# The first block's second map by seven over quarter blocks, its sums of weights made once, and opening loads in 4 KB rows

## The chip, the cores and the metric

The kernel runs on one core of one Trainium2 chip. The metric is the device time of one execution in microseconds (us). The kernel before took 1738.44 us as the median of three runs, from 1736.94 to 1740.64.

## What is computed

One decoder layer on x of 1 x 2048 x 1024 in float32: a token-mixing half (one input projection, a short causal convolution on one part, causal pooling over four windows on the other, one output projection), then an MLP with squared ReLU, each half with a DeepNorm residual and a LayerNorm, and each modulated by a vector that comes from c.

```python
mod = silu(c) @ w_ada + b_ada            # sh1, sc1, g1, sh2, sc2, g2
h = x * (1 + sc1) + sh1
z = h @ w_in
mix = concat(gate_b * short_conv(gate_c * v_conv), pool(v_pool)) @ w_out
x = layer_norm(ALPHA * x + (1 + g1) * mix)
h = x * (1 + sc2) + sh2
f = square(relu(h @ w_mlp_in)) @ w_mlp_out      # 1024 -> 4096 -> 1024
x = layer_norm(ALPHA * x + (1 + g2) * f)
```

The first map of the MLP is `w_mlp_in`, the second is `w_mlp_out`.

## The kernel before

**Tiling.** The 2048 tokens are two blocks of 1024 (b = 0 and 1). Every operand of a matmul is split into a high part in fp32r and a low part that holds the rest, and `mm3` (L84 to L87) makes three matmuls of it: high by high, high by low, low by high. So one tile step of a product costs three matmuls of 128 x 512 (L85, L86, L87). The split is one cast on ScalarE (ACT, L80) and one subtraction on VectorE (DVE, L81). Products of blocks are made by the scheme of Winograd's seven: seven products of half blocks in the place of eight, on operands that are sums and differences of blocks. Those sums are made on DVE (L90), and those of weights are kept in DRAM.

**Stages.** The stages follow one another: the opening (loads, modulation of the first k), the input projection of block 0 (`first_group`, L392, then the rest), its output projection, its first map (`up`, eight groups g of seven products each), its second map (`down`), and then the same for block 1.

**The first map.** Each group of `up` (L964) issues seven products. A product has 24 matmuls, 12 for each of two PSUM banks. The products go to three pairs of banks, X, Y and Z. Product 0 writes X. Then `keep` (L973, two ACT copies of 128 x 512) takes X into the tile c11. Product 2 then adds to X, and `keep` takes it into c12, product 4 adds to X once more. Products 1 and 5 write Y or Z and are added with `add` to what was kept (L90 on DVE, two adds of 128 x 512). `join` puts ReLU (L982) and square (L983) on ACT behind that. What results goes to DRAM (`usum`, L989, by GpSimd's queue, POOL), in block 1 also as the sums of its quarter blocks: `save_quarters` (L946), four DVE sums of 128 x 256 and three stores (L952, L954, L959) into `uquart`, done for two of the tiles of each group. All these tiles come from one pool, o, of ten slots; in block 0 one of them holds the conditioning row until the second map, so nine turn round.

**Sums of weights.** Between the groups of `up`, `sum_blocks` (L930) and `sum_weights` (L500) make sums of weights for later stages, a half at a time: four loads of 256 KB into two o tiles, four DVE sums of 128 x 512, four stores of 256 KB. `HALF_SUMS` says how many half-sums stand behind each group of block 0. Block 1 makes eight more, one behind each group (into `wquart`, L941).

**The second map.** `down` (L1068) takes the seven products in steps of half a product (96 matmuls of 512 columns). In block 0 it has all seven products as 14 such steps. In block 1 products 1 and 5 are left out of these steps, and each is made by seven again over quarter blocks (14 products of 48 matmuls of 256 columns in all, L1104), from `uquart` and `wquart`. Beside the steps of block 0 stand the sums of the next block's inputs (`sum_x`), the residual, and the gate row g2 (`row_of`).

**What sets the order.** A scheduler puts the instructions of every engine into one fixed order, by priority and by the pool slots that it expects to be free; an engine executes its list in that order and waits at the head of it. SyncE (SP) issues the loads in order, POOL the stores. At the start, `in_turn` (L97) chains the opening loads, the conditioning vector is spread over the partitions by eight transposes (L133), seven warm-up matmuls follow (L146), `ada_first` (L175) makes the modulation of k = 0, and `shifted` (L208) applies it on ACT.

## Time and profile before

| what | value |
|---|---|
| median of three runs | 1738.44 us (1736.94 to 1740.64) |
| profiled execution | 1739.93 us, of which the span is 1738.1 us |
| mean granted clock of TensorE | 0.997 |
| TensorE (PE) busy | 1721.4 us, 99% of the span |
| DVE, ACT, POOL busy | 77%, 51%, 13% |
| DMA | 479.42 MB, mean 276 GB/s |

Busy times say how full an engine was, not what the end waited for. Here PE is full from one end to the other, so a change in the time is either fewer or shorter matmuls, or a change in the few places where PE stands. For those the list of waits by engine and line is read, and for the cause of one the timeline of the engine that it waited for. Times in a timeline are from the start of the span.

### The profile page before, as it was taken

The numbers are of one execution on the slowest core, as the hardware profiler recorded it, in microseconds if no ns is written. First come the engines' busy times: TensorE is split into PE (matmuls) and PEld (weight loads), VectorE is DVE, ScalarE is ACT, GpSimd is POOL, SyncE is SP. The second block draws the span as 40 slices with busy tenths as digits, with TensorE's granted clock in tenths as the row PEclk, the third lists the DMA queues.
The fourth block names the chain that finished last, engine by engine and source line by source line (L and its number), as shares of the span: only waits on it lengthen the run. The fifth ranks groups of instructions, "written<-read, shape, count | busy, mean of one in ns | idle before, by whom it ended". The sixth has DMA issues, their size and how long they took to land.

```text
span 1738.1 us, 22312 instructions
## 1 busy us (share of the span) xinstructions
PE 1721.4 (99%) x7966; PEld 1438.7 (83%) x7966; DVE 1341.7 (77%) x1753; ACT 880.1 (51%) x1190; POOL 232.6 (13%) x437
## 2 busy tenths in 40 slices
PE   8999999999999999999999999999999999999997
PEld 7888888888888888888888888887888888998886
DVE  7898697877777686669686789687767768887885
ACT  5323358554445555446573344774545555773551
POOL 0212221112232000000000000103222221000000
PEclk9999999999999999999999999999999999999999
DMA  9898877778888999787672366557765589998871
GB/s 376 320 337 324 313 251 276 257 276 304 321 328 312 382 419 342 291 301 245 214 261 79 117 226 214 209 197 270 252 247 200 212 311 393 381 359 330 282 254 49
DMA packets 149583, 479.42 MB, mean 276 GB/s; under 512 B 17632, under 2 KB 18144, under 8 KB 149472
## 3 DMA queue, kind: packets, MB, share of 16 engines
q1 hardware_dynamic: 102816, 313.88, 50.1%
q0 software_dynamic: 46656, 164.13, 24.7%
q8 instruction: 62, 1.02, 0.2%
q14 instruction: 49, 0.40, 0.1%
HBM read 328.51 MB, written 149.42 MB: 275 GB/s over the span
## 4 chain that ended last, share of the span: by engine, by line
PE 93%; issue 2%; DMA 2%; DVE 1%; ACT 0%; POOL 0%; SPq 0%; DVEq 0%; POOLq 0%; ACTq 0%
PE ps L85 28%; PE ps L86 28%; PE ps L87 28%; PE ps L1104 5%; PE ps L392 3%; PE ps L743 1%; DMA usum<-o 1%; DVE o L90 1%; DMA r<-in_w 0%; DMA o<-in_wins 0%; DMA r<-in_win 0%; DVE o L1300 0%; DVE o L1294 0%; DMA w2sum<-o 0%; DVE st L712 0%
## 5 line engine op out<-in xcount | busy, mean ns | idle before, releaser
L85 PE MATMUL ps<-h,w 128*128 128x512 f32 x1312 | 510.1, 389 | 1.4 <-ACT o L973 1.4
L87 PE MATMUL ps<-h,w 128*128 128x512 f32 x1312 | 510.3, 389 | 0.1
L86 PE MATMUL ps<-h,w 128*128 128x512 f32 x1312 | 510.3, 389 | 0.0
L85 PE MATMUL ps<-h,h 128*128 128x512 f32 x992 | 386.3, 389 | 0.0
L87 PE MATMUL ps<-h,h 128*128 128x512 f32 x992 | 386.1, 389 | 0.0
L86 PE MATMUL ps<-h,h 128*128 128x512 f32 x992 | 386.0, 389 | 0.0
L80 ACT CAST h<-r 128x1024 fp32r<-128x1024 f32 (+1 forms) x196 | 199.3, 1021 | 283.5 <-PE ps L86 143.5
L81 DVE TENSOR_TENSOR h<-r,h 128x1024 fp32r<-128x1024 f32 (+1 forms) x196 | 230.8, 1182 | 83.9 <-ACT h L80 81.0
L85 PEld LDWEIGHTS ps<-h,w 128*128 128x128 f32 x1312 | 246.0, 188 | 53.3 <-ACT o L973 1.8
L87 PEld LDWEIGHTS ps<-h,w 128*128 128x128 f32 x1312 | 246.2, 188 | 51.6 <-DVE w L81 0.5
L86 PEld LDWEIGHTS ps<-h,w 128*128 128x128 f32 x1312 | 246.3, 188 | 51.5 <-DVE h L81 0.5
L80 ACT CAST w<-r 128x1024 fp32r<-128x1024 f32 x156 | 164.1, 1052 | 236.7 <-PE ps L86 230.4
L81 DVE TENSOR_TENSOR w<-r,w 128x1024 fp32r<-128x1024 f32 x156 | 190.4, 1221 | 78.9 <-ACT w L80 78.6
L90 DVE TENSOR_TENSOR o<-o,o 128x1024 f32<-128x1024 f32 (+2 forms) x218 | 186.6, 859 | 52.4 <-DMA usum<-o 45.4
L87 PEld LDWEIGHTS ps<-h,h 128*128 128x128 f32 x992 | 186.2, 188 | 38.9
L85 PEld LDWEIGHTS ps<-h,h 128*128 128x128 f32 x992 | 186.2, 188 | 38.7 <-DVE o L862 0.2
L86 PEld LDWEIGHTS ps<-h,h 128*128 128x128 f32 x992 | 186.2, 188 | 38.4
L81 DVE TENSOR_TENSOR h<-w,h 128x1024 fp32r<-128x1024 f32 x124 | 151.2, 1219 | 9.0 <-ACT h L80 9.0
L90 DVE TENSOR_TENSOR o<-o,ps 128x512 f32<-128x512 f32 (+1 forms) x172 | 111.7, 664 | 40.7 <-PE ps L87 39.8
L80 ACT CAST h<-w 128x1024 fp32r<-128x1024 f32 x124 | 130.1, 1049 | 12.1 <-DMA w<-in_w 7.1
L989 POOL DMA_DIRECT2D usum<-o x96 | 51.4, 536 | 419.4 <-DVE o L90 144.5
L90 DVE TENSOR_TENSOR r<-r,r 128x1024 f32<-128x1024 f32 x60 | 73.4, 1223 | 28.3 <-DMA r<-in_w 25.3
(145 smaller groups left out, 1419.0 us busy)
## 6 DMA issues: line engine op xcount, KB each, us to landing
usum<-o POOLq DMA_DIRECT2D x96, 512.0 KB, 5.5
r<-usum SPq DMA_DIRECT2D x96, 512.0 KB, 5.6
w<-w2sum SPq DMA_DIRECT2D x64, 512.0 KB, 6.3
r<-in_w SPq DMA_DIRECT2D x60, 512.0 KB, 6.0
o<-in_w SPq DMA_DIRECT2D x72, 256.0 KB, 6.5
w2sum<-o POOLq DMA_DIRECT2D x64, 256.0 KB, 6.6
w<-in_w SPq DMA_DIRECT2D x32, 512.0 KB, 6.6
r<-uquart SPq DMA_DIRECT2D x28, 512.0 KB, 6.0
```

Of the source, the lines that this page charges most:

```text
L80: high = nc.scalar.copy(hi, src)
L81: return high.ins, nc.vector.tensor_tensor(lo, src, hi.bitcast(F32), op=ALU.subtract).ins
L85: nc.tensor.matmul(ps, whi, xhi, start=first, stop=False, skip_group_check=goes_on)
L86: nc.tensor.matmul(ps, whi, xlo, start=False, stop=False, skip_group_check=goes_on)
L87: nc.tensor.matmul(ps, wlo, xhi, start=False, stop=last, skip_group_check=goes_on)
L90: return nc.vector.tensor_tensor(out_, a, b_, op=op)
L392: nc.tensor.matmul(ps[m, h], wt[:, w : w + P], A[k][p // 2][:, hs], start=k == 0 and p == 0, stop=k == KD - 1 and p == 2)
L743: nc.tensor.transpose(ps[:, t * P : t * P + P], R[4 * h + t][:, k * P : k * P + P], ident)
L989: nc.gpsimd.dma_start(usum[g, i], r)
L1104: nc.tensor.matmul(ps, a[:, us], w[:, gs], start=not begun, stop=hf == 1 and g == 3 and a is ul, skip_group_check=True)
```

## The change

Four things are changed.

1. Block 0's second map takes the form of block 1's: ten steps for products 0, 2, 3, 4 and 6, and 14 products over quarter blocks (L1122 now) for products 1 and 5. So block 0's first map saves quarter sums too, and the work beside the steps (residual, `sum_x`, `row_of`) moves to earlier steps.
2. The eight half-sums of `wquart` are made once, in block 0's first map, and block 1 makes none.
3. The opening loads are three of 512 KB with rows of 4 KB, from a new input `opening` that the host lays out, and one of 256 KB. Before they were seven of 256 KB with rows of 2 KB. `ada_first` goes by halves of the row.
4. Four warm-up matmuls on zeros stand ahead of the spread of the conditioning vector, and 14 behind it (seven before).

The diff, cut to its core:

```diff
-HALF_SUMS = (1, 2, 3, 3, 3, 3, 3, 0)
-WARM = 7
+HALF_SUMS = (2, 3, 4, 4, 4, 4, 4, 1)
+EARLY, WARM = 4, 14
...
-    for hs in halves:
-        for i, f in enumerate((SC1, SH1)):
-            in_turn(first[i][:, hs], wada[f][:, hs])
-    in_turn(w0[:, :H], win0[0])
-    for hs in halves:
-        in_turn(x0[:, hs], xT[0, 0][:, hs])
+    for r, src in zip((first[0], first[1], w0), opening):
+        in_turn(r, src)
+    in_turn(x0[:, H:], xT[0, 0][:, H:])
+    zeros = t_tmp()[:, :P]
+    nc.vector.memset(zeros, 0.0)
+    warm = t_ps()
...
+    warming(EARLY)
...
-    warm = t_ps()
-    for _ in range(WARM):
-        nc.tensor.matmul(warm[:, :P], ident, ident, start=True, stop=True)
+    with tc.issue_after(spreads[-1]):
+        warming(WARM)
...
         def save(r, i):
-            if fine and i in (1, 7):
+            if i in (1, 7):
                 save_quarters(r, i // 4, g)
...
-        coarse = (0, 2, 3, 4, 6) if b else (0, 1, 2, 3, 5, 4, 6)
-        steps = [(i, hf) for i in coarse for hf in range(2)]
+        steps = [(i, hf) for i in (0, 2, 3, 4, 6) for hf in range(2)]
...
-            if b and n == 1:
+            if n == 1:
                 made = [fine_operands(*todo[m]) for m in range(2)]
...
-            if n == base:
+            if n == 2:
                 next(later)
-            if base <= n < base + 4:
+            if 2 <= n < 6:
                 later.send(ready[1])
...
-            if b == 0 and n == 4:
+            if b == 0 and n == 2:
                 row_of(g2, mod[:, G2 : G2 + KD])
...
-        else:
-            sums = [(sum_blocks, [w2q[n, i, hf] for i in range(4)], wquart[n, hf], p)
-                    for n in range(2) for hf in range(2) for p in halves]
+            sums += [(sum_blocks, [w2q[n, i, hf] for i in range(4)], wquart[n, hf], p)
+                     for n in range(2) for hf in range(2) for p in halves]
...
-            some = 1 if b else HALF_SUMS[g]
+            some = HALF_SUMS[g]
```

**How the instructions move.** The first place is ACT's list in block 0's first map, group g = 4. The names: o_571 is c11 of this group before, o_579 its c12, o_584 its c22; w_580, w_585 and w_587 are the high parts of the weights of products 3, 4 and 5, and a w tile's slot comes free when an earlier product has been made. Before:

```order
L80 CAST w_580_3803<-r_576_3767 128x1024 [waits PE_49]
L973 COPY o_571_3729<-ps_569_3703 128x512 [waits DMASW4_49,DVE_49]
L973 COPY o_571_3729<-ps_570_3716 128x512 [waits PE_49]
L982 ACTIVATE o_571_3729<-o_571_3729 128x1024 [waits DVE_49]
L80 CAST w_585_3836<-r_565_3693 128x1024 [waits PE_49]
L983 ACTIVATE o_571_3729<-o_571_3729 128x1024 [waits Activation_49]
L973 COPY o_579_3800<-ps_569_3703 128x512 [waits DMASW6_49,PE_49]
L80 CAST w_587_3869<-r_564_3692 128x1024 [waits PE_49]
L973 COPY o_579_3800<-ps_570_3716 128x512 [waits PE_49]
```

In the changed kernel o_588 is c11 of the same group, o_596 its c12 and o_601 its c22, and w_597, w_602 and w_604 belong to products 3, 4 and 5:

```order
L80 CAST w_597_3925<-r_593_3889 128x1024 [waits PE_49]
L80 CAST w_602_3958<-r_582_3815 128x1024 [waits DVE_49,PE_49]
L80 CAST w_604_3991<-r_581_3814 128x1024 [waits DVE_49,PE_49]
L982 COPY o_588_3851<-ps_586_3825 128x512 [waits DMASW5_49,DMASW3_49,DVE_49]
L982 COPY o_588_3851<-ps_587_3838 128x512
L982 COPY o_596_3922<-ps_586_3825 128x512 [waits DMASW5_49,DMASW4_49,DMASW6_49,DVE_49,PE_49]
L982 COPY o_601_3955<-ps_599_3929 128x512 [waits DMASW6_49,DMASW7_49,DMASW0_49,DVE_49]
L982 COPY o_601_3955<-ps_600_3942 128x512
L991 ACTIVATE o_588_3851<-o_588_3851 128x1024 [waits DVE_49]
L80 CAST w_607_4030<-r_583_3816 128x1024 [waits DMAHW6_49,PE_49]
L992 ACTIVATE o_588_3851<-o_588_3851 128x1024 [waits Activation_49]
L982 COPY o_596_3922<-ps_587_3838 128x512 [waits PE_49]
```

The copies that free X for product 2 have moved from ahead of the casts for products 4 and 5 to behind them, and the second copy of c12, which frees X for product 4, now stands behind ReLU and square of c11. The cast of w_604 waits for the end of product 3. PE's list has turned round with it: in groups 2 to 7 it makes the products in the order 0, 1, 3, 2, 4, 5, 6, before in the order 0 to 6. The same rows in the same order stand in groups 3 to 7.

The second place is DVE's list in the same group of the changed kernel, the last rows ahead of what the ReLU of c11 waits for (the second row of o_588). The tiles o_576 to o_579 are half-sums of weights, the low part of product 5's weights is w_605, and ps_591 and ps_592 are the banks of Y:

```order
L90 TENSOR_TENSOR o_576_3785<-o_576_3785 128x512 [waits DMAHW1_49,DMAHW0_49,DMASW4_49]
L81 TENSOR_TENSOR w_605_3992<-r_581_3814,w_604_3991 128x1024 [waits PE_49,Activation_49]
L90 TENSOR_TENSOR o_576_3785<-o_576_3785,o_577_3786 128x512 [waits DMAHW2_49,DVE_49]
L90 TENSOR_TENSOR o_588_3851<-o_588_3851,ps_591_3858 128x512 [waits DMASW3_49,Activation_49]
L90 TENSOR_TENSOR o_577_3786<-o_576_3785,o_577_3786 128x512 [waits DMASW7_49,DMASW6_49,DVE_49]
L90 TENSOR_TENSOR o_578_3799<-o_578_3799 128x512 [waits DMAHW5_49,DMAHW4_49,DMASW0_49]
L90 TENSOR_TENSOR o_577_3786<-o_577_3786 128x512 [waits DMAHW3_49,DVE_49]
L90 TENSOR_TENSOR o_578_3799<-o_578_3799,o_579_3800 128x512 [waits DMAHW6_49,DVE_49]
L90 TENSOR_TENSOR o_588_3851<-o_588_3851,ps_592_3871 128x512 [waits Activation_49]
```

From the quarter sums of the group before (the tile o_571) to the last of these rows there are 18 DVE instructions in a row: 14 sums of half-sums, two low parts of weights, and the two adds. Before, the adds of c11 stood among such sums too, but product 3 stood between the copies of c12 and product 4, which needs them; now product 4 follows product 2 at once.

The third place is the head of PE's list, up to the first matmul of the input projection (L392 before, L401 now). Before:

```order
L133 MATMUL ps_94<-ident,silu 128x128 x4
L133 MATMUL ps_99<-ident,silu 128x128 x4
L146 MATMUL ps_104<-ident 128x128 x7
L392 MATMUL ps_184<-h_161,w_160 128x512
L392 MATMUL ps_186<-h_161,w_160 128x512
```

And now:

```order
L119 MATMUL ps_79<-tmp_77 128x128 x4
L141 MATMUL ps_98<-ident,silu 128x128 x4
L141 MATMUL ps_103<-ident,silu 128x128 x4
L119 MATMUL ps_79<-tmp_77 128x128 x14
L401 MATMUL ps_194<-h_171,w_170 128x512
```

Seven more matmuls stand between the spread and the first matmul of the input projection, and four ahead of the spread.

More of the change, by code (lines that the diff above doesn't have):

```diff
@@ L42, in tile_hybrid_layer @@
 @with_exitstack
-def tile_hybrid_layer(ctx: ExitStack, tc: tile.TileContext, xT, x, wada, vec, win0, win,
+def tile_hybrid_layer(ctx: ExitStack, tc: tile.TileContext, opening, xT, x, wada, vec, win0, win,
                       wins, wpool, wout, wmix, w1, w2, w2q, rows, out):
@@ L109, in tile_hybrid_layer, with warming @@
     w0 = t_r()
-    for hs in halves:
-        for i, f in enumerate((SC1, SH1)):
-            in_turn(first[i][:, hs], wada[f][:, hs])
-    in_turn(w0[:, :H], win0[0])
-    for hs in halves:
-        in_turn(x0[:, hs], xT[0, 0][:, hs])
+    for r, src in zip((first[0], first[1], w0), opening):
[4 more added lines that the diff above has]
+    warm = t_ps()
+    def warming(n):
+        for _ in range(n):
+            nc.tensor.matmul(warm[:, :P], zeros, zeros, start=True, stop=True)
+    warming(EARLY)
     silu = cp.tile([P, KD], F32, name="silu")
@@ L1233, in down @@
             banks, new, then = table[i]
-            matmuls(banks, ops, new, hf == 0, hf == 1, then, hf == 1 and i in by_tile)
-            if b and n == 1:
+            matmuls(banks, ops, new, hf == 0, hf == 1, then, hf == 1 and i in (3, 4, 6))
+            if n == 1:
                 for m, (k, part_) in enumerate(todo):
@@ L1331, in mlp @@
     def mlp(b, B, back, g2):
-        ups = [up(g, B, b == NB - 1) for g in range(NC)]
+        ups = [up(g, B) for g in range(NC)]
         for g in range(2):
```

52 lines of the change are left out of this document (26 added, 26 removed).

## The prediction

> **What bounds the kernel now.** I read the page's engine shares first, then PE's waits by releaser, then the chain and the timelines of the places named there.
>
> ```profile
> span 1738.1 us, 22312 instructions
> PE 1721.4 (99%) x7966; PEld 1438.7 (83%) x7966; DVE 1341.7 (77%) x1753; ACT 880.1 (51%) x1190; POOL 232.6 (13%) x437
> ```
>
> PE's waits (microseconds in total, times, longest):
>
> ```profile
> PE ps L133 <- DVE silu L90: 3.1, 1, 3.1
> PE ps L392 <- ACT h L209: 3.0, 1, 3.0
> PE ps L85 <- ACT o L973: 1.4, 1, 1.4
> ```
>
> PE is full, and the three waits sum to 7.5 us: two in the opening, one in block 1. So little is to be won beside matmuls saved, and any new wait of PE counts in full. The third wait shows the kind. Its PE rows, then ACT's rows (start, length, what, idle before and its releaser), then the row of the chain that holds block 1's quarter products:
>
> ```profile
> 1180.75 0.39 PE L85 MATMUL ps<-h,w 128*128 128x512 f32 x1
> ...
> 1183.93 0.39 PE L87 MATMUL ps<-h,w 128*128 128x512 f32 x1
> 1185.71 0.50 PE L85 MATMUL ps<-h,w 128*128 128x512 f32 x1 [1.40 <-ACT o L973]
> ```
>
> ```profile
> 1184.13 1.04 ACT L80 CAST w<-r 128x1024 fp32r<-128x1024 f32 x1 [4.38 <-PE ps L86]
> 1185.08 2.04 ACT L973 COPY o<-ps 128x512 f32<-128x512 f32 x4
> ```
>
> ```profile
> 1474.33 80.63 PE ps L1104 x672
> ```
>
> Fourteen steps from 1180.75 to 1183.93 are 0.227 us a matmul. Then 1.78 pass to the next start, so 1.56 are lost: a cast that waits for the end of product 3 stands ahead of the copy that frees the bank, and the copy starts only behind it.
>
> **The change part by part.** The sum is made on the profiled execution, 1739.93 us (span 1738.1 and 1.8 around it). That is 1.5 above the median of the runs, so my prediction takes the sum's difference from 1738.4.
>
> *Quarter products in block 0.* Products 1 and 5 leave as 4 steps of 96 matmuls: 384 x 0.227 = 87.2 us. In come 672 matmuls of 256 columns, 80.6 by the row of L1104. PE is the bound there, so **-6.5**.
>
> *Opening.* PE's rows, ACT's rows, and three stretches (PE, PEld, DVE, ACT, POOL busy, granted clock, DMA share, GB/s):
>
> ```profile
> 4.83 2.28 PE L146 MATMUL ps<-ident 128*128 128x128 f32 x14
> 10.14 22.19 PE L392 MATMUL ps<-h,w 128*128 128x512 f32 x84 [3.03 <-ACT h L209]
> ```
>
> ```profile
> 9.27 1.52 ACT L209 ACTIVATE h<-o,mod 128x512 fp32r<-128x512 f32 x2
> 15.10 1.52 ACT L209 ACTIVATE h<-o,mod 128x512 fp32r<-128x512 f32 x2 [1.48 <-DVE mod L191]
> ```
>
> ```profile
> 4.00:6.00 2.00, 2.00 (x11) 2.00 (x10) 1.39 (x4) 0.00 (x0) 0.00 (x0) 1.00 0.74 211
> 12.00:14.00 2.00, 2.00 (x6) 1.60 (x5) 2.00 (x4) 0.62 (x1) 0.00 (x0) 0.50 1.03 419
> 16.00:18.00 2.00, 2.00 (x10) 1.61 (x9) 1.46 (x3) 2.00 (x4) 0.00 (x0) 0.94 1.04 422
> ```
>
> The opening's 2 KB rows moved 211 GB/s, the 4 KB rows of the later loads 419. So the modulation should be ready about a microsecond earlier. But PE has 14 warm-up matmuls now in the place of 7: 4.83 + 2 x 2.28 = 9.39 is the earliest start of the input projection, 0.75 before 10.14. After PE's gap of 3.03 the clock was at half, still so from 12 to 14, and near full again from 16 on: the first 84 matmuls took 22.19 where 84 x 0.227 = 19.1, so 3.1 were lost. With PE busy from the spread on I expect the full clock. What is late next is k = 1: its ACT step stood at 15.10, and product 0 would end at 9.39 + 24 x 0.227 = 14.8; with loads a microsecond earlier it is up to 0.6 late. So -0.75 - 3.1 + 0.5 = **-3.3**, bounds -0.7 (no clock gained) and -3.9.
>
> The Trainium skill ("TensorE: Matmul & The Clock Gate", Part 1, What's actually happening) says that the clock falls after an idle window of about 3.4 us, and that the window runs free. The trace differs: a gap of 3.03, shorter than a window, halved it. By the page's rule 3.03 would have cost nothing and the half clock came from the phase, so the change might keep it: the sum would be 3.1 higher.
>
> *Block 1's first map.* Eight half-sums less. PE is the bound, so only the wait above can go; there the copy now stands ahead of the cast. **-1.4**, bounds -1.6 and 0.
>
> *Block 0's first map.* This is the large term. The same order that cost 1.56 once now stands in five groups, g = 3 to 7: casts for products 4 and 5, then the copies of c11, while product 2, which needs them, follows product 3. So 1.56 a group is the least. The second copy of c12, which the second half of product 4 needs, is later still. For it I walk one group on rows of block 1 (same saves, one half-sum) and then of block 0, group 4. T is the start of the cast for product 2, which the last matmuls of the group before release; products end at T + 5.44 each.
>
> ACT, DVE and POOL of a group in block 1:
>
> ```profile
> 1316.38 1.06 ACT L80 CAST w<-r 128x1024 fp32r<-128x1024 f32 x1 [1.85 <-PE ps L86]
> ...
> 1321.82 1.05 ACT L80 CAST w<-r 128x1024 fp32r<-128x1024 f32 x1 [2.80 <-PE ps L86]
> ```
>
> ```profile
> 1323.94 1.23 DVE L90 TENSOR_TENSOR o<-o,o 128x1024 f32<-128x1024 f32 x1 [3.18 <-DMA usum<-o]
> 1325.09 1.22 DVE L81 TENSOR_TENSOR w<-r,w 128x1024 fp32r<-128x1024 f32 x1
> 1326.22 0.76 DVE L90 TENSOR_TENSOR o<-o 128x256 f32<-128x256 f32 x2
> 1326.89 0.88 DVE L90 TENSOR_TENSOR o<-o,o 128x256 f32<-128x256 f32 x2
> 1327.69 1.28 DVE L90 TENSOR_TENSOR o<-o,ps 128x512 f32<-128x512 f32 x2
> 1328.89 0.69 DVE L90 TENSOR_TENSOR o<-o 128x512 f32<-128x512 f32 x1
> 1329.49 1.22 DVE L81 TENSOR_TENSOR w<-r,w 128x1024 fp32r<-128x1024 f32 x1
> 1330.62 1.41 DVE L90 TENSOR_TENSOR o<-o,o 128x512 f32<-128x512 f32 x2
> ```
>
> ```profile
> 1326.17 0.58 POOL L954 DMA_DIRECT2D uquart<-o  x1
> ```
>
> Issues by kind in the DMA view of 1310 to 1350 (KB each, median us to landing), and ACT of block 0, group 4:
>
> ```profile
> o<-in_w2q SPq DMA_DIRECT2D x4, 256.0 KB, 7.0
> uquart<-o POOLq DMA_DIRECT2D x2, 128.0 KB, 5.8
> ```
>
> ```profile
> 429.97 1.06 ACT L80 CAST w<-r 128x1024 fp32r<-128x1024 f32 x1 [1.18 <-PE ps L86]
> ...
> 445.25 1.06 ACT L982 ACTIVATE o<-o 128x1024 f32<-128x1024 f32 x1 [7.27 <-DVE o L90]
> 446.22 1.03 ACT L80 CAST w<-r 128x1024 fp32r<-128x1024 f32 x1
> 447.15 1.06 ACT L983 ACTIVATE o<-o 128x1024 f32<-128x1024 f32 x1
> 448.12 0.56 ACT L973 COPY o<-ps 128x512 f32<-128x512 f32 x1
> ```
>
> The last subtraction on c11 waits for a store and starts at T + 7.6, and the quarter sums end at 1327.69 = T + 11.3. Behind them the new order has 14 sums and two adds of 128 x 512 (0.60 from 1328.89 to 1329.49) and two low parts (1.13 from 1329.49 to 1330.62): 16 x 0.60 + 2 x 1.13 = 11.9, so the last add ends at T + 23.2 if its loads are there. The last pair of loads needs the slot of the tile whose quarter store is issued at 1326.17 (T + 9.8): + 5.8 + 7.0 = T + 22.6, with two DVE steps behind it T + 23.8. Then ReLU, cast, square and copy, 445.25 to 448.68 = 3.4: the copy ends at T + 27.2. Without any wait PE would want that bank at T + 21.8 + 2.7 = T + 24.5. So 2.7 a group, and more as the DMA fills: I take 3.0, between 1.56 and 5.
>
> ```profile
> 409.00:447.00 38.00, 37.94 (x168) 31.08 (x166) 27.89 (x33) 17.22 (x21) 9.76 (x20) 1.00 0.83 306
> ```
>
> Each more half-sum adds 2.1 MB, the quarter saves 0.7: 306 + 2.8 MB / 38 us = 380 GB/s, share 1.0, where the opening's later stretch moved 419. Five groups make 15. Group 1 has block 1's pattern, 1.56, and group 2, with three half-sums, I put at 1.5 (0 to 3). **+18**, bounds +8 (five times 1.56, nothing in groups 1 and 2) and +29.
>
> The Trainium skill ("DMA: Bandwidth & Descriptors", Specifications) gives a core about 358 GB/s from HBM; the trace does not hold to it (419). By 358 each of the five groups would take 38.1 x 380 / 358 = 40.4 at least, 2.3 more, which lies below the wait found above and would change no sign.
>
> *Block 0's second map.* Four of its steps have the loads of `sum_x` and of the residual together now; before, these stood beside different steps. A step of block 0 with `sum_x` and one of block 1 with the residual:
>
> ```profile
> 626.00:648.00 22.00, 22.00 (x99) 18.22 (x98) 16.93 (x19) 12.45 (x15) 1.07 (x2) 1.00 1.03 418
> 1577.00:1599.00 22.00, 22.00 (x98) 18.21 (x98) 16.58 (x16) 8.27 (x9) 1.07 (x2) 1.00 0.91 330
> ```
>
> `sum_x` adds 2.1 MB in 22 us to the 330 GB/s of the second row: 425, as full as the first, where PE was busy throughout. At 419 a step would be 0.3 us longer, and loads land later; **+1**, bounds 0 and +4 (one us a step).
>
> Sum: -6.5 - 3.3 - 1.4 + 18 + 1 = +7.8, so 1747.7 by the profiled execution and **1746.2** by the median. A measurement of this kernel can't tell less than about 0.2% (3.5 us) from no change.
>
> **The rivals.** *The cover holds (0.21).* If the DVE row is through earlier than I walked it, the wait behind the cast is the only one left: 5 x 1.56 = 7.8 and -6.5 - 3.3 - 1.4 + 7.8 = -3.4, 1735; if in some groups the casts run before product 3 ends, down to 1727. That is faster than before. It decides at T + 22.6: a ReLU of c11 that starts by then adds nothing to the 1.56. For it speaks that in block 0 before, c11's ReLU started at 445.25, T + 15.3; against it, that the quarter sums and the fourth half-sum (1.47 + 4 x 0.60, and the subtraction behind a store) stand ahead of it now, and that the cast for product 5 cannot start before product 3 ends.
>
> *DMA-bound first map (0.15).* With share 1.0 stores and loads land 2 to 3 us later each; both stand in the chain above, so 5 a group and more: 25 + 6 + 4 - 11.2 = +24, 1762. It decides where groups 3 to 7 move above 400 GB/s.
>
> *No clock gained in the opening (0.12).* If the half clock comes again, the opening gives 0.7, and the sum is +10.4, 1749. The Trainium skill ("TensorE: Matmul & The Clock Gate", Part 1, What's actually happening) would allow it by the phase of its window.
>
> **How the numbers follow.** The forecast (waits of 2 to 4 us in five groups, 1738 to 1753) has 0.52, of which 0.14 lies within 0.2% (up to 1741.9). The first rival's 0.21 is 0.04 within it and 0.17 below 1734.9. So faster 0.17, same 0.18, and slower 0.38 + 0.15 + 0.12 = 0.65. The range of 1733 to 1758 leaves out some 0.1 of the first rival and 0.1 of the second.
>
> **What would show it.** In the profile after: a wait of PE (L85) on ACT's copy (L982), five to seven times, some 15 us in all; groups 3 to 7 of block 0's first map 40 to 42 us long; the quarter products twice at 80.6; the first matmul of the input projection at 9.4 and the clock at 1.00 until 20 us; no such wait in block 1. The prediction is wrong if PE shows no wait on L982, or if those groups are 38.1 us long.

## The result and the profile after

| kernel | us, median (lowest to highest) | runs |
|---|---|---|
| before | 1739.54 (1736.94 to 1741.67) | 4 |
| after | 1807.06 (1800.47 to 1808.37) | 4 |

The ratio is 1.0381 with a 95% interval of 1.0351 to 1.0412: the changed kernel is slower by 67.5 us, where I had forecast 7.8. The page of the changed kernel (profiled execution 1808.23 us, mean granted clock 0.982), then PE's waits (microseconds in total, times, longest):

```profile
span 1806.3 us, 23209 instructions
PE 1741.8 (96%) x8276; PEld 1463.6 (81%) x8276; DVE 1399.7 (77%) x1858; ACT 905.2 (50%) x1222; POOL 257.4 (14%) x469
```

```profile
PE ps L85 <- ACT o L982: 40.2, 12, 5.2
PE ps L86 <- DVE h L81: 6.3, 1, 6.3
PE ps L1112 <- ACT o L1122: 3.9, 1, 3.9
```

Before, the three longest waits of PE came to 7.5 us. Now one line has 40.2 us in twelve waits, two in each of groups 3 to 7 where the prediction had one. Cut at the starts of PE's stages in the two timelines, the 68.3 us between the two profiled executions lie here:

| stage | before | after | difference |
|---|---|---|---|
| up to the end of the input projection's first part | 56.65 | 53.42 | -3.2 |
| from there to the first map of block 0 | 231.57 | 231.33 | -0.2 |
| first map of block 0 | 294.48 | 358.09 | **+63.6** |
| second map of block 0 | 305.53 | 315.14 | **+9.6** |
| block 1, of which its first map -1.7 | | | -1.5 |

**The opening.** PE's first row of the input projection, and the first two of the stretches that the prediction showed of before (PE, PEld, DVE, ACT, POOL busy, granted clock, DMA share, GB/s):

```profile
9.38 0.73 PE L401 MATMUL ps<-h,w 128*128 128x512 f32 x2 [1.47 <-ACT h L217]
```

```profile
4.00:6.00 2.00, 2.00 (x19) 2.00 (x18) 1.01 (x3) 0.00 (x0) 0.00 (x0) 1.00 0.92 356
...
12.00:14.00 2.00, 2.00 (x11) 1.62 (x10) 2.00 (x3) 0.49 (x1) 0.00 (x0) 1.00 1.02 418
```

The input projection starts at 9.38, after a wait of 1.47, and the clock from 12 to 14 is 1.00 where it was 0.50: the part of the change that the prediction had right.

**A group of the first map.** Group 4, walked as in the prediction, with T = 449.48. ACT, DVE, the quarter store on POOL, and PE (start, length, what, idle before and its releaser):

```profile
449.48 1.06 ACT L80 CAST w<-r 128x1024 fp32r<-128x1024 f32 x1 [1.84 <-PE ps L86]
...
465.80 1.04 ACT L80 CAST w<-r 128x1024 fp32r<-128x1024 f32 x1 [4.38 <-PE ps L86]
469.03 1.07 ACT L982 COPY o<-ps 128x512 f32<-128x512 f32 x2 [2.18 <-DMA uquart<-o]
...
479.72 1.06 ACT L991 ACTIVATE o<-o 128x1024 f32<-128x1024 f32 x1 [2.96 <-DVE o L90]
480.69 1.03 ACT L80 CAST w<-r 128x1024 fp32r<-128x1024 f32 x1
481.62 1.05 ACT L992 ACTIVATE o<-o 128x1024 f32<-128x1024 f32 x1
482.58 0.56 ACT L982 COPY o<-ps 128x512 f32<-128x512 f32 x1
```

```profile
457.48 1.23 DVE L90 TENSOR_TENSOR o<-o,o 128x1024 f32<-128x1024 f32 x1 [3.61 <-DMA usum<-o]
...
466.08 1.42 DVE L90 TENSOR_TENSOR o<-o,o 128x512 f32<-128x512 f32 x2 [0.38 <-DMA o<-in_w]
467.83 0.69 DVE L90 TENSOR_TENSOR o<-o 128x512 f32<-128x512 f32 x1 [0.34 <-DMA o<-in_w]
471.29 0.69 DVE L90 TENSOR_TENSOR o<-o 128x512 f32<-128x512 f32 x1 [2.77 <-DMA o<-in_w]
...
477.19 1.29 DVE L90 TENSOR_TENSOR o<-o 128x512 f32<-128x512 f32 x2 [2.27 <-DMA o<-in_w]
...
479.01 0.68 DVE L90 TENSOR_TENSOR o<-o,ps 128x512 f32<-128x512 f32 x1
```

```profile
461.61 0.75 POOL L968 DMA_DIRECT2D uquart<-o  x1 [1.32 <-DVE o L90]
```

```profile
434.18 0.68 PE L85 MATMUL ps<-h,w 128*128 128x512 f32 x1 [3.66 <-ACT o L982]
469.67 0.80 PE L85 MATMUL ps<-h,w 128*128 128x512 f32 x1 [3.68 <-ACT o L982]
483.20 0.50 PE L85 MATMUL ps<-h,w 128*128 128x512 f32 x1 [2.47 <-ACT o L982]
629.09 0.50 PE L85 MATMUL ps<-h,w 128*128 128x512 f32 x1 [1.70 <-ACT o L982]
```

The first wait ends at 469.67, when the copies of c11 have run: they waited for a slot that a quarter store gave back 7.4 us after its issue. The second ends at 483.20, behind the second copy of c12, and that chain reads backwards: copy 482.58, square, cast, ReLU 479.72, the last add of c11 at 479.01, and ahead of it on DVE sums of weights that stood 0.38 + 0.34 + 2.77 + 2.27 = 5.8 us for their loads. From 434.18 (group 3) to 629.09 (group 7) the same place comes four groups later: 194.91 / 4 = 48.7 us a group, against 38.1 without waits.

Where the loads stood is seen in SP's list; the last experiments below test it. SP's issues around the group, with the DMA view's row for its half-sum loads (KB each, us to landing) and two stretches:

```profile
420.42 32.34 SPq L497 DMA_DIRECT2D r<-in_w  x4
452.86 3.00 SPq L514 DMA_DIRECT2D o<-in_wins  x4
455.96 12.12 SPq L944 DMA_DIRECT2D o<-in_w  x12
```

```profile
o<-in_w SPq DMA_DIRECT2D x12, 256.0 KB, 10.3
```

```profile
430.00:450.00 20.00, 16.34 (x66) 13.03 (x65) 15.29 (x17) 10.68 (x12) 3.54 (x7) 0.91 0.46 184
...
465.00:485.00 20.00, 13.85 (x49) 10.58 (x48) 11.42 (x17) 7.10 (x10) 7.76 (x15) 0.83 1.04 413
```

The fourth load of L497 is the first weights (a11) of the next group, far ahead of its use. It stands at the head of SP's list until 452.4, and the 16 half-sum loads behind it are issued only from 452.9 on, when the DMA has been half idle for 20 us (184 GB/s), and then crowd at 413 GB/s.

**The second map.** Its two waits in the list above, 6.3 and 3.9 us, have their causes on two engines. In the longer one PE waits for a low part while DVE is full with the normalisation, the residual and the gate row, which now stand beside fewer steps. In the other it waits for a copy of a quarter product that stands on ACT behind a row of casts, the first of which waited for a load of quarter sums. The stretch of the first, and ACT's row of the second:

```profile
884.00:906.00 22.00, 15.49 (x57) 11.93 (x56) 20.53 (x31) 16.15 (x29) 1.06 (x2) 0.84 0.89 311
```

```profile
692.93 1.05 ACT L80 CAST h<-r 128x1024 fp32r<-128x1024 f32 x1 [5.24 <-DMA r<-uquart]
```

### The profile page after: what moved, and what is told of

The parts are those of the page before. It is cut to its first block, busy times and chain, and to the rows that moved or that the text cites. A ratio compares the mean times of both kernels' runs of the same rounds, so it can differ in the third digit from the quotient of the medians.

```text
span 1806.3 us, 23209 instructions
## 1 busy us (share of the span) xinstructions
PE 1741.8 (96%) x8276; PEld 1463.6 (81%) x8276; DVE 1399.7 (77%) x1858; ACT 905.2 (50%) x1222; POOL 257.4 (14%) x469
## 4 chain that ended last, share of the span: by engine, by line
PE 45%; DVE 3%; DMA 1%; ACT 1%; issue 1%; DVEq 0%; ACTq 0%
PE ps L86 13%; PE ps L87 13%; PE ps L85 13%; PE ps L1112 4%; DVE h L81 1%; DVE o L90 1%; DMA r<-in_wins 1%; DVE o L1294 1%; DMA r<-usum 0%; PE ps L752 0%; DVE o L1300 0%; DVE o L1284 0%; DMA r<-winsum 0%; ACT h L601 0%; ACT w L80 0%
## 5 line engine op out<-in xcount | busy, mean ns | idle before, releaser
L85 PE MATMUL ps<-h,w 128*128 128x512 f32 x1312 | 519.5, 396 | 40.2 <-ACT o L982 40.2
L87 PE MATMUL ps<-h,w 128*128 128x512 f32 x1312 | 516.4, 394 | 2.5 <-DVE w L81 2.5
L86 PE MATMUL ps<-h,w 128*128 128x512 f32 x1312 | 517.2, 394 | 0.0
L86 PE MATMUL ps<-h,h 128*128 128x512 f32 x864 | 337.0, 390 | 6.3 <-DVE h L81 6.3
L87 PE MATMUL ps<-h,h 128*128 128x512 f32 x864 | 337.0, 390 | 0.0
L85 PE MATMUL ps<-h,h 128*128 128x512 f32 x864 | 336.8, 390 | 0.2 <-ACT h L80 0.2
L85 PEld LDWEIGHTS ps<-h,w 128*128 128x128 f32 x1312 | 250.4, 191 | 97.6 <-ACT o L982 45.3
L80 ACT CAST h<-r 128x1024 fp32r<-128x1024 f32 (+1 forms) x208 | 212.0, 1023 | 233.5 <-PE ps L86 87.1
L87 PEld LDWEIGHTS ps<-h,w 128*128 128x128 f32 x1312 | 250.4, 191 | 56.6 <-DVE w L81 3.4
L86 PEld LDWEIGHTS ps<-h,w 128*128 128x128 f32 x1312 | 250.9, 191 | 52.6 <-DVE h L81 0.5
L81 DVE TENSOR_TENSOR h<-r,h 128x1024 fp32r<-128x1024 f32 (+1 forms) x208 | 245.6, 1185 | 56.4 <-ACT h L80 56.2
L90 DVE TENSOR_TENSOR o<-o,o 128x512 f32<-128x512 f32 (+2 forms) x250 | 200.6, 803 | 59.4 <-DMA usum<-o 48.6
L86 PEld LDWEIGHTS ps<-h,h 128*128 128x128 f32 x864 | 162.8, 188 | 40.7 <-DVE h L81 6.7
L85 PEld LDWEIGHTS ps<-h,h 128*128 128x128 f32 x864 | 162.7, 188 | 34.1 <-ACT h L80 0.6
L87 PEld LDWEIGHTS ps<-h,h 128*128 128x128 f32 x864 | 162.8, 188 | 33.7
L81 DVE TENSOR_TENSOR h<-w,h 128x1024 fp32r<-128x1024 f32 x136 | 165.9, 1220 | 11.1 <-ACT h L80 10.5
L1112 PE MATMUL ps<-h,h 128*128 128x256 f32 x1344 | 164.2, 286 | 3.9 <-ACT o L1122 3.9
L1112 PEld LDWEIGHTS ps<-h,h 128*128 128x128 f32 x1344 | 164.0, 195 | 4.3 <-ACT o L1122 4.1
L80 ACT CAST h<-w 128x1024 fp32r<-128x1024 f32 x136 | 142.8, 1050 | 19.8 <-DMA w<-in_w 8.2
```

The source lines that it names most:

```text
L80: high = nc.scalar.copy(hi, src)
L81: return high.ins, nc.vector.tensor_tensor(lo, src, hi.bitcast(F32), op=ALU.subtract).ins
L85: nc.tensor.matmul(ps, whi, xhi, start=first, stop=False, skip_group_check=goes_on)
L86: nc.tensor.matmul(ps, whi, xlo, start=False, stop=False, skip_group_check=goes_on)
L87: nc.tensor.matmul(ps, wlo, xhi, start=False, stop=last, skip_group_check=goes_on)
L90: return nc.vector.tensor_tensor(out_, a, b_, op=op)
```

## The experiments

The theory from this trace: the first map is held by a loop through the nine slots of the pool o (a store lands, a slot comes free, a load of a half-sum is issued and lands, DVE sums in its order, c11 is added, ACT copies, PE goes on). The rivals: the order of cast and copies on ACT, which my prediction had priced; the bytes on the DMA; the half clock that follows each wait. The length of block 0's first map, cut as in the table at the starts of PE's stages, tells them apart: 294.5 us before, 358.1 after. Times with an interval are from several runs; the others are single runs, beside 1739 to 1741 for the kernel before. The four runs of the changed kernel lie 8 us apart, so a few us between two single runs say nothing.

**One addition at a time.** The changed kernel without the eight half-sums of `wquart` (so the quarter products use raw quarters of the weights):

```diff
-HALF_SUMS = (2, 3, 4, 4, 4, 4, 4, 1)
+HALF_SUMS = (1, 2, 3, 3, 3, 3, 3, 0)
...
-                nc.sync.dma_start(q, wquart[n, hf, int(w) - 1] if len(w) == 1 else
+                nc.sync.dma_start(q, w2q[n, int(w) - 1, hf] if len(w) == 1 else
```

> The changed kernel without the eight half-sums of wquart in block 0's first map (the half-sums per group are again 1, 2, 3, 3, 3, 3, 3, 0); both second maps then read unsummed blocks of the weights in their place, so that the output is not the reference's. The quarter saves of block 0 stay. In the changed kernel block 0's first map took 357.9 us where it took 294.5 before, with 44.6 us of PE waits and some 19 us of lost clock. Theory A (order: casts that wait for product 3 stand ahead of the copies of c11): the cast for product 5 is behind the copies in this kernel's list, so the waits on the copies should all but vanish: map of 294 to 303 us. Theory B (slots: the nine o tiles do not turn round fast enough, since the quarter saves hold theirs until a store has landed): three half-sums and the saves still need more tiles than before; some waits stay, map of 305 to 330. Theory C (bytes: the DMA is full while half-sums and saves overlap): a quarter of the added bytes stays, map of 300 to 315.

1757.78 us; the map takes 323.3, the second map 299.6. And the changed kernel without the quarter saves in block 0 (its quarter products load whole tiles, so without the sums of quarters):

```diff
-            if i in (1, 7):
+            if b and i in (1, 7):
                 save_quarters(r, i // 4, g)
...
-                nc.sync.dma_start(r, uquart[n, UQ[a], hf])
+                nc.sync.dma_start(r, uquart[n, UQ[a], hf] if b else usum[4 * hf + UQ[a] // 2, 1 + 6 * n])
```

> The changed kernel without the quarter saves of block 0: its first map stores those tiles whole, and its second map's quarter products read such whole tiles, so that the output is not the reference's. All 26 half-sums stay. In this kernel's list the copies of c11 stand ahead of the casts for products 4 and 5 again, and PE makes the products in the order 0 to 6. Theory A (order): no wait on the copies of c11, map of 294 to 300 us. Theory B (slots): the saves' two tiles a group and the store that the last of them waits for are gone, so the same, 294 to 303. Theory C (bytes): most of the added bytes (8 half-sums, 17 MB against 6 MB of the saves) stay, so waits of 20 us and more stay, map of 315 to 345.

1762.51 us; map 324.0, where I had put the bytes, and not the slots. So the half-sums alone cost 29.5 and the saves alone 28.8, together 58.3 of the 63.6: neither is the culprit, and nothing shows of a threshold that only both would pass. PE's waits in the two maps:

```profile
PE ps L87 <- DVE w L81: 11.0, 5, 5.6
PE ps L85 <- ACT o L981: 9.4, 5, 3.5
```

```profile
PE ps L85 <- ACT o L982: 10.1, 5, 3.9
PE ps L87 <- DVE w L81: 8.2, 5, 3.3
```

In both, half of it is a wait for a low part of weights, a kind that the prediction did not have. The second map of 299.6 against 305.5 is the gain of the quarter products, -5.9 where I had -6.5.

**The order on ACT.** The cast for product 3 put behind the copies of c11:

```diff
         else:
-            product(3, Z, True)
+            with tc.issue_after(kept[1]):
+                product(3, Z, True)
```

> The changed kernel with one edge more in the order: the cast for product 3 stands behind the copies of c11, so that ACT's list has the copies ahead of the casts for products 3, 4 and 5 as before the change, and PE makes the products in the order 0 to 6. All work stays. Theory A (order): the waits fall to below 10 us, map of 295 to 310 us. Theory B (slots): the copies of c11 still wait until the quarter store of the group before has landed, some 19 us into the group, where product 2 now needs them at 11; so the first wait of a group grows from 3 to 4 us to 7 to 9 and the second one shrinks: map of 335 to 375, no better. Theory C (bytes): no fewer bytes, so no better either, 340 to 370.

1834.6 us; map 393.4, above every range that I had given, and the longest of the waits:

```profile
PE ps L85 <- ACT o L983: 49.4, 7, 8.6
```

The scheduler's turned order was no mistake: product 3 filled part of the wait for the slot. The order alone, to which the prediction gave the least price, is refuted as the cause.

**One slot more.** In block 0 the pool keeps one slot for the conditioning row; here it is given back, with the modulation of the gate row g2 left out:

```diff
-                ada(G2 + 4 * n, G2 + 4 * n + 4, nc.sync.dma_start, lambda: t_o(D))
+                nc.vector.tensor_tensor(mod[:, G2 + 4 * n : G2 + 4 * n + 4], acc[:, G1 + 4 * n : G1 + 4 * n + 4],
+                                        vecs[:, G1 + 4 * n : G1 + 4 * n + 4], op=ALU.add)
```

> The changed kernel with ten o slots in block 0's first map in the place of nine: the conditioning row that holds the tenth is not kept for the gate g2, whose eight loads and dots at the head of the second map are left out (g2 is made from the sums of another gate, so the output is not the reference's). The half-sums, the saves and the order of PE's products stay as in the changed kernel. Slots: the waits of block 0's first map (44.6 us, map 357.9 us) fall by a third or more, map below 340. Bytes: the same bytes pass in that map, so it stays at 350 to 362; only the second map gets shorter, by the loads left out.

1798.66 us; map 363.0. The same two waits on PE's timeline:

```profile
467.90 0.50 PE L85 MATMUL ps<-h,w 128*128 128x512 f32 x1 [1.39 <-ACT o L982]
483.70 0.80 PE L85 MATMUL ps<-h,w 128*128 128x512 f32 x1 [7.35 <-ACT o L982]
```

The first wait falls from 3.68 to 1.39, and the second grows from 2.47 to 7.35. PE goes on at 483.70 where it was 483.20: the group is set by the late chain through DVE, and the first wait only takes its share of it. The second map fell to 301.1. Its waits do not hang on the row g2 alone, though: with g2's work it took 299.6 above and 301.0 with the half-sums' loads on POOL below. Why they come in some runs and not in others stays open.

**Bytes.** The kernel before with the new opening (taken apart below), with eight copies from DRAM to DRAM of 256 KB added to each of groups 1 to 7, and then the same with half the bytes:

```diff
+        if g and not fine:
+            for i, j in enumerate((0, 3, 4, 6)):
+                nc.sync.dma_start(scrap[g, 0, i], usum[g - 1, j][:, :H])
+                nc.gpsimd.dma_start(scrap[g, 1, i], usum[g - 1, j][:, H:])
```

> The kernel before with the new opening (1735.96 us) and bytes added that need no slot and no DVE: in groups 1 to 7 of block 0's first map eight copies of 256 KB each from DRAM to DRAM, four on the queue of the loads and four on that of the stores, as many transfers and bytes as one half-sum has. It computes the same. Bytes: one half-sum more a group cost 29.5 us where the quarter saves were left out, so 15 to 30 us here too, map of 309 to 324. Slots: no tile is held longer than a somewhat later landing makes it, 0 to 6 us, map of 294 to 300.

> The kernel of the run with bytes alone, with each added copy cut to 128 KB (half the rows, rows as long as before); number, place and waits of the copies are the same. There block 0's first map took 341.8 us against 293.9 with the opening alone, 47.9 more. If the bytes on the DMA engines make that time, half of it or less is left (a part of them fits into the idle stretches): map of 300 to 320. If it is the number of transfers and their waits at the head of the two queues, the map stays at 335 to 345.

1784.15 us (map 342.0) and 1780.02 (335.9). Halving the bytes took 6 of 48 us away, so this cost was not the bytes either. SP's waits in the second show what it was, and that the pair is a poor test of bytes:

```profile
SPq L1016 <- DMA usum<-o: 119.0, 18, 16.1
```

My copies read tiles that had just been stored; SP stood at its head for the stores, and the loads behind came late. It was by accident the first sign of what held the changed kernel.

**The clock.** Eleven small matmuls in each of the two waits of groups 2 to 7 (`busy(n)` makes n matmuls of 128 columns on the identity):

```diff
-            product(3, Z, True)
+            last = product(3, Z, True)
+            if b == 0 and g > 1:
+                with tc.issue_after(last):
+                    busy(FILL)
...
-        product(4, X, False)
+        product(4, X, False, FILL if b == 0 and g > 1 else 0)
```

> The changed kernel with eleven matmuls on the identity (some 3.6 us) put into each of the two waits of groups 2 to 7: behind product 3, ahead of product 2, and between the two banks of product 4. The order of all else stays. If the 19 us that block 0's first map lost beside its waits are the half clock after each wait, the fillers keep the clock full and win most of it: map of 338 to 347 in the place of 357.9, granted clock of the span up from 0.982 to 0.99 or more. If the loss is something else (late operands, bank access), the map stays at 356 to 365.

1805.21 us. The mean clock rose from 0.982 to 0.992, and half-rate matmuls in the map fell from 74 to 32, but the quarter products start at 686.93 where they started at 686.36. In this run, then, what the half clock cost was hidden in the next wait: nothing of the loss came back with the clock.

**The opening, taken apart.** The new opening alone on the kernel before, then its warm-ups alone, then its loads alone (with seven warm-ups as before):

```diff
-WARM = 7
+EARLY, WARM = 4, 14
...
+    for r, src in zip((first[0], first[1], w0), opening):
+        in_turn(r, src)
```

> The kernel before with the opening of the changed kernel alone (loads in 4 KB rows, 4 and 14 warm-up matmuls), nothing else. The input projection should start at 9.4 and its first part end 3 us earlier, as in the changed kernel; nothing behind it should move. By the time of the changed kernel's stages (first part 53.4 against 56.65): 3 to 4 us below the kernel before, ratio 0.9977 to 0.9983. If the gain depends on the phase of the clock's window, some runs show none and the median lies 1 to 3 below.

> The kernel before with the warm-up matmuls alone (4 ahead of the spread, 14 behind it), loads as before. The modulation is as late as before, so the input projection starts at 10.1 us; the clock, at half there before, stays full, so its first part ends some 2 us earlier: 1.5 to 3 us below the kernel before. If the clock was not the larger part of the opening's 3.5 us, it is below 1.

> The kernel before with the loads in 4 KB rows and the new order of the first sums alone, seven warm-up matmuls behind the spread as before and none ahead of it. The input projection starts at 8.5 to 9.4 us, since fewer warm-ups stand ahead of it, but after PE's idle gap of 1.5 to 2.5 us the clock may fall to half again: 0.5 to 2.5 us below the kernel before. If the shorter gap leaves the clock full, 3 to 4.5 below, better than both together.

| kernel | us | ratio to before (95%) | input projection starts, first part ends |
|---|---|---|---|
| whole opening | 1735.96, 11 runs | 0.9981 (0.9972 to 0.9990) | 9.35, 53.39 |
| warm-ups alone | 1737.87, 10 runs | 0.9991 (0.9981 to 1.0000) | 10.50, 54.54 |
| loads alone | 1736.07, 10 runs | 0.9984 (0.9974 to 0.9993) | 9.04, 53.13 |

```profile
4.00:6.00 2.00, 2.00 (x11) 2.00 (x10) 1.07 (x3) 0.00 (x0) 0.00 (x0) 1.00 1.01 393
```

The new loads (512 KB in rows of 4 KB) run at 393 GB/s (loads alone, row above) where the old ones ran at 211; size and row length changed together here. That makes the modulation ready so much earlier that PE's gap is 0.90 us and the clock stays full with seven warm-ups too. Each half alone keeps the clock: from its start to the end of the first part the input projection takes 44.0 to 44.1 us in all three, and 46.5 before. The loads also start it 1.1 us earlier, the warm-ups alone 0.4 later. The whole opening on the kernel before is the version that beats both, by 0.2%.

**The half-sums behind c11.** The full work of the change, with the sums of each group placed on DVE behind the adds of c11 in the next group; then the same with the tenth slot (g2's modulation left out):

```diff
-        join(c11, Y)
+        joined = join(c11, Y)
...
+        if g:
+            making(g, joined)
         product(4, X, False)
```

> The changed kernel with all its work, but with each group's half-sums put behind the sum of c11 on DVE, inside the next group, in the place of ahead of it; so DVE's list has the two adds of c11 ahead of every sum that waits for a load, and ACT's list has the ReLU of c11 ahead of the copy of c12 that waits for product 2. If the second wait of each group (on the copy of c12) is the sums' loads, met by DVE in order ahead of c11's adds, that wait goes and block 0's first map falls from 357.9 us to 310 to 335, with only waits on the slots of c11 left. If it is the slots or the transfers as such, the waits move to other tiles and the map stays at 345 to 370.

> The run before with the tenth o slot as well (the work for the gate g2 at the head of the second map left out, so the output is not the reference's). With the sums behind c11 the slots should be what is left: the map falls by 10 us or more below that of the run with nine slots. If nine slots were enough there, the two maps are within 4 us.

1797.72 us (four runs, 1.0336, 1.0318 to 1.0353) with a map of 344.8, and 1774.44 with 332.8. (The maps of 340 and 323.5 us in the expectations end at the last matmul; PE then stands another 4.2 and 8.9 us for the first operands of the second map. Their weights stand on SP behind loads of half-sums, so this counts in the map.) The wait on ACT's copies is nearly gone, and waits for low parts stand in its place (first kernel, then the second):

```profile
PE ps L87 <- DVE w L81: 27.1, 7, 8.5
```

```profile
PE ps L87 <- DVE w L81: 17.9, 6, 6.2
```

DVE's order is worth 13 us of the map and 9 of the whole, much less than I had expected: the map is nearly in the range that I had for slots or transfers. The slot is worth 12 us of the map on top of it. The slot that did nothing in the changed kernel counts as soon as DVE's order does not hold the group.

**SP's list.** Some 38 us still had no cause. In the changed kernel and in the two just shown, the half-sums' loads were given to POOL:

```diff
-                nc.sync.dma_start(r, src[i][:, p])
+                nc.gpsimd.dma_start(r, src[i][:, p])
```

> The changed kernel, with the loads of all half-sums issued by GpSimd (POOL) in the place of SyncE (SP). In the changed kernel the first map of block 0 takes 358.1 us, SP stands 122.6 us in five waits at loads of first-map weights (L497), and the half-sums' loads behind them land 10.3 us after issue. Theory one, SP's one list in order is a limb of the loop: the half-sums' loads no longer stand behind loads of weights, the waits of PE on ACT's copy (L982) fall from 40 us in twelve to under 30, and the map takes 330 to 348. Theory two, the tiles of the pool o and the stores that free them set the loop, whoever issues: the loads now wait at the head of POOL's list and hold the stores behind them, and the map takes 355 or more.

> The kernel whose half-sums stand behind the adds of c11 (map 340 us, 27.1 us of waits of PE on low parts of weights), with the loads of the half-sums issued by POOL in the place of SP. There SP stood 146.4 us in 18 waits at loads of weights, and the half-sums' loads behind them came late, with DVE waiting for them ahead of the low part that PE needed. Theory one, SP's list: PE's waits on low parts fall to under 12 us and the map takes 315 to 328. Theory two, slots and stores: the waits stay above 20 us and the map takes 336 or more.

> The kernel with the half-sums behind the adds of c11 and ten slots (the modulation of the gate row g2 is left out; map 323.5 us, 17.9 us of waits on low parts), with the half-sums' loads issued by POOL. In its group from 426 us SP issued nothing between 427.3 and 448.5, standing at a load of weights, and then ten half-sum loads between 457.4 and 467.7; DVE waited for such loads ahead of the low part. Theory one, SP's list: this is most of what is left above 294.5 us, and the map takes 298 to 312. Theory two, DVE's order and the extra work themselves: the map stays above 318.

1887.94, 1810.99 and 1797.61 us; maps of 446.6, 344.6 and 340.9. All three kernels are slower, and no map is shorter (the second is as it was). In the first, the loads now landed sooner (5.2 us, the median from 325 to 570, against 8.4) and yet the map was 88 us longer, so the landing time was not the cause. But the test settled nothing on SP, since POOL's list held the loads behind its stores. So the next three move one load on SP instead: a11 of the next group goes behind the group's half-sum loads.

```diff
+            behind = last_load.pop(g - 2, None) if i == 0 else None
+            with tc.issue_after(behind) if behind else nullcontext():
-            nc.sync.dma_start(r, src[i])
+                nc.sync.dma_start(r, src[i])
```

> The changed kernel with one load moved on SP in each group of block 0's first map: the first weights of the next group (a11, L497), which stood ahead of the group's 16 half-sum loads, is issued behind them. In group 4 of the changed kernel SP issued three such loads from 420 us on, then stood at that one until 452.4, and only then issued the 16 half-sum loads; the DMA moved 88 to 240 GB/s meanwhile and 411 to 420 afterwards. Theory one, this load at the head of SP's list is what makes the half-sums late: they are issued 10 us and more earlier, DVE no longer stands 5.8 us a group at them, the group falls from 48.7 us to 41 to 44, and the map from 358 to 310 to 335. Theory two, the half-sums' loads would have had to wait for their slots anyway: the map stays above 345.

> The same move in the kernel whose half-sums stand behind the adds of c11 (map 340 us). Theory one: SP's 146 us of waits at weights go, PE's 27 us on low parts fall under 12, and the map takes 300 to 322. Theory two: the map stays above 332.

> The same move in the kernel with the half-sums behind c11 and ten slots (the modulation of the gate row g2 is left out; map 323.5 us). Theory one: most of what is left above 294.5 goes, the map takes 296 to 310. Theory two: it stays above 317, and what is left lies in DVE's order or in the extra work itself.

In the changed kernel: 1781.13 us, map 334.1, 24 us shorter by the place of one load. DVE's waits from 325 to 570, ACT and DVE in group 4 (the cast that is T and the second copy of c12; the last add of c11), SP's issues, and SP's waits from 325 to 570:

```profile
DVE r L90 <- DMA r<-in_w: 20.1, 5, 6.0
...
DVE o L90 <- DMA o<-in_w: 2.2, 2, 1.7
```

```profile
438.17 1.06 ACT L80 CAST w<-r 128x1024 fp32r<-128x1024 f32 x1 [0.93 <-PE ps L86]
...
465.49 0.58 ACT L988 COPY o<-ps 128x512 f32<-128x512 f32 x1
```

```profile
461.46 0.68 DVE L90 TENSOR_TENSOR o<-o,ps 128x512 f32<-128x512 f32 x1
```

```profile
430.91 2.09 SPq L520 DMA_DIRECT2D o<-in_wins  x4
438.12 17.50 SPq L950 DMA_DIRECT2D o<-in_w  x12
```

```profile
SPq L950 <- DMA w2sum<-o: 49.4, 8, 13.6
SPq L950 <- DMA usum<-o: 49.2, 12, 7.9
```

In the changed kernel DVE's row on half-sum loads was 25.2 us in 19 waits and SP's on L497 122.6 in five:

```profile
DVE o L90 <- DMA o<-in_w: 25.2, 19, 2.9
```

```profile
SPq L497 <- DVE o L90: 122.6, 5, 27.2
```

The cast that is T stands at 438.17 here. So the first four half-sum loads go at T - 7.3 and the others from T, where they went from T + 3.4 and T + 6.5, and DVE hardly waits for them any more (2.2 us). The last add of c11 ends at T + 24.0 and the copy at T + 27.9, near the T + 23.2 and T + 27.2 of the prediction. In PE's timeline the second waits of groups 3 to 7 fall from 16.8 us in all to 2.3, while the first waits stay (17.9 and 17.2): in groups 4 to 6 the copies of c11 still wait for stores that free slots. A group takes 45.1 us, one more than the range that I had for it. SP now waits for stores into the slots of o, the next limb of the loop, and DVE for the weights that go later (20.1 us, before 9.8).

In the other two kernels the move brought nothing (1803.28 and 1779.58 us, maps of 346.4 and 342.2): SP stood at the slots of o in place of the weights, and PE waited for the weights all the same (for their casts in the first, 20.9 us in six waits, for their low parts in the second, 25.1 in seven).

Shown, then: SP's early load (24 of the 64 us in the changed kernel), DVE's order (13) and, behind it, the slots (12). They are limbs of one loop and do not add up; no version with all the work came under 334 us. Of the 40 us that are left there, PE's waits make 28, 24 of them for ACT's copies into o. Whether these go with more slots was not tried, and the rest was not taken apart: both stay open.

## Why the prediction was right or wrong

**The opening, the quarter products, block 1: right.** -3.2 in the changed kernel and -3.5 alone, where I had -3.3, with the start at 9.38 as worked out; -5.9 where nothing disturbs the second map (I had -6.5); -1.7 in block 1's first map, with no wait on L982 there (I had -1.4). The new loads alone bring the whole gain; the warm-ups alone bring the clock's part of it. The prediction left that undivided. The Trainium skill ("TensorE: Matmul & The Clock Gate", Part 1, What's actually happening) allowed the half clock to stay by the window's phase; in the profiled runs with the new opening, or with either half of it, it went every time.

**Block 0's first map: the direction right, the size wrong; +18 forecast, +63.6 measured.** The term was mis-sized in the walk of one group. Its first half nearly held: the subtraction on c11 starts at T + 8.0 (I had 7.6) and the quarter store is issued at T + 12.1 (9.8). What failed is "the last add ends at T + 23.2 if its loads are there", with the last loads put at T + 22.6. They were there at T + 27.7, the add ended at T + 30.2 and the copy at T + 33.7, not T + 27.2. Against T + 24.5, when PE would want the bank, that makes 9.2 a group and not 2.7; the profile shows 48.7 us a group, 10.6 above 38.1. I had taken the landing time of four loads in block 1 (7.0 us), where nothing crowds, and let each load go when its own slot came free. I did not walk SP's list: there the half-sums' loads of a group stand behind one load of the next group's weights, SP executes in order, and that load waits until T + 3. The list of SP in the changed kernel shows this place; the prediction read ACT's, DVE's and PE's. The upper bound of 5 a group was drawn from the DMA's bandwidth, which was not what was late. With that one load moved, the walk nearly held (T + 24.0 and T + 27.9), and 24 of the 46 us above the forecast map of 312 went. The other 22 are not this step's, and their cause is open in part: the first wait of a group, put at 1.56, was 1.4 to 5.4 us there too.

**Two waits a group.** I had priced one wait of PE a group; in groups 3 to 7 there are two, on two limbs of the loop. The tenth slot shortened the first and the second grew; the load moved on SP took the second away and left the first. The slots hold the first, the late sums on DVE the second.

**Groups 1 and 2** cost the rest, some 10 us (63.6 less five times 10.6) where I had 3.1.

**Block 0's second map: +1 forecast, and 15.5 measured** (315.1 against 299.6 where no wait stood). I had priced the DMA's fullness beside the steps; what showed was DVE, full beside fewer steps, and a late load of quarter sums ahead of ACT's copies. The bound of 4 counted neither. These waits are no fixed price of the new form: in the runs with all the work the second map took from 301 to 325 us.

**The rivals.** That the cover holds was refuted (twelve waits). The DMA-bound map came nearest with 1762, and the stretch from 465 to 485 did run above 400 GB/s, its point of decision; but 184 GB/s stood ahead of it, and with one load moved on SP the same bytes took 24 us less. Full bandwidth was a mark of loads let go late, not the limit. No clock gained in the opening: refuted.

## What to carry to other kernels

A change that adds loads to a full software pipeline has to be walked on the list of the engine that issues them, with its order: one early load that waits for a slot holds every load behind it, and the DMA is idle and then crowded in the same group. When the pool's slots turn round in a loop, the cost of extra work is the length of the loop and not its engine time, and each limb that is mended shows the next. Where a wait is seen in two places of a group, take each of them away by itself before adding them up. And measure a stage from its first matmul to the first of the next stage, or a wait at the border is lost.

## What the runs showed of the hardware

The half clock does not go by the length of a wait alone. In the changed kernel:

```profile
337.17 0.50 PE L85 MATMUL ps<-h,w 128*128 128x512 f32 x1 [3.01 <-ACT o L982]
337.51 0.40 PE L86 MATMUL ps<-h,w 128*128 128x512 f32 x1
...
383.45 0.79 PE L85 MATMUL ps<-h,w 128*128 128x512 f32 x1 [2.52 <-ACT o L982]
384.04 0.63 PE L86 MATMUL ps<-h,w 128*128 128x512 f32 x1
```

After 3.01 us of waiting the second matmul starts 0.34 us behind the first and takes 0.40, after 2.52 us 0.59 and 0.63: the clock was kept over the longer wait and halved over the shorter one. The Trainium skill (the same page and section) says that the window runs free, and this pair agrees that the phase counts; its "≥1 idle window (~3.4µs)" does not fit a wait of 2.52.
